# Layer one's values' pair and narrow gate pair side by side, both by seven products

## The chip, the core and the metric

The kernel runs on one core of one Trainium2 chip. The metric is the device time of one execution in microseconds (us), the median of the runs. Engine names are those of the profile: PE is the matmul engine (PEld its weight loads), DVE the vector engine, ACT the scalar engine, POOL and SP two engines that here mostly issue transfers.

## The reference

Two layers of a hybrid streaming encoder on 512 tokens of width 2048, all in float32. The changed part is the input projection of the first layer: some column blocks of `h @ w_in`.

```python
def hybrid_layer(x, w_in, w_out, g_pre, g_post, w_alpha, b_alpha, g_gla, g_att, rel_bias):
    h = rmsnorm(x, g_pre)
    z = h @ w_in
    gq, gk, gv, gg, ga, aq, ak, av, ag = split_columns(z)
    log_a = jax.nn.log_sigmoid((ga @ w_alpha + b_alpha).astype(jnp.float32)) / GLA_TAU
    ...
    o_att = chunk_band_attention(aq..., ak..., av..., rel_bias)
    o_att = rmsnorm(o_att, g_att...) * jax.nn.silu(ag)
    y = jnp.concatenate([o_gla, o_att], axis=-1) @ w_out
    return x + rmsnorm(y, g_post)
```

`av` (1024 columns) are the attention's values, `ag` (1024 columns) its gates, `ga` (16 columns) feed the forget gate.

## The kernel before

**Tiling.** The inner dimension of 2048 is cut into 8 chunks of 256 (two weight rows of 128, index `kk`), the tokens into 4 tiles of 128. The gates `ag` are one full block AG0 of 512 columns and two narrow blocks AG1 and AG2 of 264, where AG2 also holds the 16 columns of `ga`. The values are the two blocks AV0 and AV1 of 512 columns.

**Two words per operand.** Each operand is kept as a high half (a rounded copy, made by ACT: `wh`, line 240, for weights; line 109 for tokens) and a low half (the rest, made by DVE: `wl`, line 250; line 110). A product is three matmuls, high x high, high x low, low x high.

**Two ways to multiply.** `std_gemm` multiplies a block directly. `fast_gemm` takes a pair of blocks and uses seven products P1 to P7 in place of eight (the Strassen-Winograd scheme): the tokens are cut into quarters A11, A12, A21, A22 (half of the tokens x half of the inner dimension), the weights into the pair's two blocks x the same halves. Sums S1 to S4 of the token quarters (`token_sums`, `make_sums`) and sums of weights are the operands of P5, P6, P3 and P7; P1, P2 and P4 use A11, A12 and A22. Each product runs over 4 chunks `c`; a line such as `PROD` lists the order, "50" being P5 of chunk 0.

**Layer one's order.** AG0 by `std_gemm` on the raw tokens; then AG1 and AG2 by `std_gemm`, while the token sums are made and written to DRAM; then the values' pair by `fast_gemm`, which fetches the sums back; then the query/key pairs QK01/QK23 and QK45/QK67. In layer two AG0 is cut in half, the values' pair is begun between the halves, and AG1/AG2 already go by seven products as `GATE_PAIR`.

**The stream.** All weights pass through one list, `stream`, of jobs (one product, one chunk). Three steps run ahead of the matmuls: `load` (a transfer issued by SP), `high` (DVE's sum or difference of weights if needed, then ACT's copy) and `low` (DVE). `ahead()` says how far: five loads, four high halves, three low halves. The tile rings behind them are `raw` (5 tiles), `wh` (4), `wl` (3) and `H` and `sa` (4 each). Each engine executes its own queue in order; waits are semaphores between engines. A transfer, too, waits in its issuer's queue until its tile is free.

**Side work.** `first_operands` makes the normed tokens and A11, A12, A21, A22 out of the raw ones (line 719 and `split`); generators in `tasks` are advanced between matmuls by `pump`, at a rate per product. `gate_evac` applies silu and writes gates to DRAM from POOL's queue.

Of the kernel before, what the change touches and what calls it, by code (L numbers as in the profile page):

```python
# [15 lines left out]
P = 128  # L16
L = 2
# [19 lines left out]
def hybrid_trunk(  # L37
# [113 lines left out]
    class Job:  # L151
        def __init__(self, l, kind, c, b0, b1=None, pair=None):
            self.l, self.kind, self.c, self.b0, self.b1, self.pair = l, kind, c, b0, b1, pair
            self.a = None
            self.parted = l == L - 1 and kind != "std" and b0 == AV0
# [18 lines left out]

        def load(self):
# [10 lines left out]
            elif k == "P1":  # L186
                h = slot(f"g{4 + c}", [2, 512]) if self.parted else rtile("H")
                p["H", self.c] = self.fetch(h, b0, top)
                last_h[0] = last_load[0]
            elif k == "P5" and self.parted:  # L190
                h = p["H", c]
                src = w[self.l, b1 - (b1 > AG1), top].rearrange("p (k n) -> p k n", k=2)
                nc.gpsimd.dma_start(h, src, accum_op=ALU.add)
            elif k == "P5":
                p["r", self.c] = self.fetch(rtile("raw", bufs=5), b1, top)
            elif k == "P6":
                p["r", self.c] = p["b22", self.c] = self.fetch(rtile("raw", bufs=5), b1, bottom)
            elif k == "P7":
                p["r", self.c] = p.pop(("t", self.c), None) or self.fetch(rtile("raw", bufs=5), b0, top)
            elif k == "P2" or (k == "P4" and (end or self.parted)):  # L200
                p["r", self.c] = self.fetch(rtile("raw", bufs=5), b0, bottom)
            sums = (so_d if end else sa_d)[self.l]
# [3 lines left out]
            else:  # L206
                home = k == "P5" and b0 == AV0
            if b0 == AG1 and k == "P5":
                p["a22", c] = slot(f"g{4 + c}", [2, 512], F32R)
                nc.sync.dma_start(flat(p["a22", c]), sums["A22", c])  # L210
            if b0 == AG1 and k == "P3":
                p["next"]["H", c] = self.fetch(slot(("g14", "g15", "g2", "g12")[c], [2, 512]), PAIRS[1][0], c)
            if b0 == AG1 and k == "P4":
                self.a = p["a22", c]
            elif src is not None and b0 != NB_IN and not home:
                until(lambda: k == "P4" or (id(sums), LEFT[k], c) in written)
                self.a = rtile("sa", (2, 512), F32R)
                with tc.issue_after(last_h[0]) if mid else nullcontext():
                    last_load[0] = nc.sync.dma_start(flat(self.a), src).ins
            if b0 == W23[0] and k == ("P6" if mid else "P5"):  # L220
# [3 lines left out]
        def high(self):  # L224
# [3 lines left out]
            else:  # L228
# [3 lines left out]
                with tc.issue_after(lows[-4 if early else -2]) if self.b0 >= NB_IN else nullcontext():  # L232
                    if k == "P6" or (k == "P5" and not self.parted) or (k == "P4" and (self.b0 >= NB_IN or self.parted)):
# [25 lines left out]
    for l in range(L):  # L259
        if l:  # L260
            pr = {}
            stream += [Job(l, "std", c, AG0) for c in CO]
# [3 lines left out]
            qk = {}  # L266
            pr = {"next": qk}
            stream += [Job(l, k, c, *GATE_PAIR, pr) for k, c in PROD_GATE]
        else:
            stream += [Job(l, "std", c, b) for b in (AG0, AG1, AG2) for c in CO]  # L270
        for b0, b1 in PAIRS[1:] if l else PAIRS:
            pr = qk if l and b0 == QK01 else {}
# [29 lines left out]
    written = set()  # L302

# [36 lines left out]
    def std_gemm(l, blk, outs, chunks, operand, evac, rate=0.0, skip=0, lag=0):  # L340
        wide = W if blk == AG0 else N1
        pss = {o: ps_mm.tile([P, W], F32, tag="mm", name=nm("mm"))[:, :wide] for o in outs}
# [29 lines left out]
    def fast_gemm(l, pair, consume, rate=0.0, skip=0, feature_major=False, after=None, end=False, lag=0, ops=A, prod=None, acc=None):  # L372
        b0 = pair[0]
        gates = b0 == AG1
        wide = N1 if gates else W
        parted = acc is not None
        if not parted:
# [6 lines left out]
        if parted:  # L384
            target.update(P5="Z", P3="Z")
        if prod is None:
# [4 lines left out]
        def copies(name, src):  # L391
            keep[name] = []
            for t in range(2):
                e = ev()[:, :wide]
# [9 lines left out]
        def finished(k, t):  # L404
# [8 lines left out]
            elif k == "P2":  # L413
                consume(0, 0, t, None, combine(acc[target[k]][t], keep["p1"][t], ALU.add, keep["p1"][t]))
            elif k == "P4":
# [35 lines left out]
        for k, c in prod:  # L451
            if k == "P2" and (end or gates) and c == 0 or k == "P5" and parted and c == 0:
                acc["Z"] = [aux()[:, :wide], aux()[:, :wide]]
            if lag and k == "P4" and c == 4 - lag:
                held = [take(l, b0, k, i) for i in range(c, 4)]
                for t in range(2):
                    with tc.issue_after(last_mm[0]) if t else nullcontext():
                        for i in range(c, 4):
                            matmuls(held[i - c], k, i, (t,))
                            pace()  # L460
                    finished(k, t)
                return
            job = take(l, b0, k, c)
            with tc.issue_after(half_turns[1]) if (k, c) == ("P4", 3) and half_turns else nullcontext():
                matmuls(job, k, c, range(2))
            ahead()
# [16 lines left out]
            pace()  # L483

# [26 lines left out]
    STAGE = ("g6", "g7", "g4", "g5", "g10")  # L511
    HOME = {("S1", c): tag for c, tag in enumerate(("g9", "g14", "g15", "g2"))}
    HOMES = {**HOME, **{("S2", c): tag for c, tag in enumerate(("g12", "g13", "g8", "g11"))}}
# [94 lines left out]
    def make_sums(dst, tags, parts, home={}):  # L608
        stage = [0]

        def sub(out, a, b):
            nc.vector.tensor_tensor(out=out, in0=a, in1=b, op=ALU.subtract)
# [13 lines left out]
        for c in range(4):  # L626
            a11, a12, a21, a22 = parts(c)
            yield
            sub(a22, a21, a22)
            put("S1", c, a22)  # L630
            yield
            sub(a21, a11, a21)
            put("S3", c, a21)
            yield
            nc.vector.tensor_tensor(out=a22, in0=a22, in1=a11, op=ALU.subtract)
            put("S2", c, a22)
            yield
            nc.vector.tensor_tensor(out=a12, in0=a12, in1=a22, op=ALU.add)
            put("S4", c, a12)
            yield  # L640

    def token_sums(l):
        tags, home = (("g10", "g16", "H", "g0", "g1"), HOMES) if l else (STAGE, HOME)
        return make_sums(sa_d[l], tags, lambda c: (full[0, c][:, 0, :], full[0, c][:, 1, :], full[1, c][:, 0, :], full[1, c][:, 1, :]), home)

    VT = ("g16", "g17", "g4", "g5", "g6", "g7", "g12", "g13")
# [59 lines left out]
    def first_operands():  # L706
        ends = []
        for ch in CO:
            kh, c = divmod(ch, 4)
            while ch not in U:  # L710
                yield
            for half in range(2):
# [4 lines left out]
                with tc.issue_after(ends[-2]) if len(ends) >= 2 else nullcontext():  # L717
                    for kk in range(2):
                        nc.vector.scalar_tensor_tensor(
                            out=dst[:, kk * 256 : (kk + 1) * 256], in0=V[ch][:, kk, tok],  # L720
                            scalar=gcol[:, 2 * ch + kk : 2 * ch + kk + 1], in1=rb[:, tok], op0=ALU.mult, op1=ALU.mult,
                        )
                if half == 0:
                    op = slot(f"a1{kh + 1}{c}", [2, 512], F32R)
                elif kh == 0:
                    op = slot(A21[c], [2, 512], F32R)
# [5 lines left out]
                if half and kh:  # L732
# [3 lines left out]
        yield from load_forget_gate(0)  # L736
# [26 lines left out]
    def load_forget_gate(l):  # L763
        raw = slot("g10" if l else "g12", [2, 512])
        fac = slot("g13", [2, 512], F32R)
# [829 lines left out]
```

## Time and profile before

| What | Value |
| --- | --- |
| Median of 3 runs | 1592.07 us (1591.72 to 1592.32) |
| The profiled execution's own time | 1594.45 us |
| Its span in the trace | 1592.7 us |
| Granted clock of PE | 0.999 |
| Narrow matmuls (264 columns) of both layers | 720 |
| First narrow gate matmul starts | 50.80 us |
| Values' pair ends, query/key pair begins | 176.68 us |
| DMA, mean over the span | 277 GB/s |

The page gives each engine's busy time and its share of the span, then the chain of work that ended last: followed back from the last instruction, at each step to what released it. Busy time of PE alone does not say how fast it works, since matmuls are pipelined: one that takes 0.28 us may be followed by the next after 0.12. So the distance from start to start is used for prices. Stretches of the trace give busy time by engine between two times.

### The profile page before, as it was taken

The page shows a single profiled execution, that of the slowest core. Times are in us where ns is not written, and L with a number is a line of the kernel's source. Part 1 is how long each engine was busy: PE and PEld are TensorE (multiplying, and loading weights), DVE is VectorE, ACT ScalarE, POOL GpSimd, SP SyncE. Part 2 cuts the span into 40 slices and gives each one's busy share as a digit, 9 for nine tenths or more (in the row PEclk, how much of TensorE's full clock was granted, in tenths as well). Part 3 has the DMA queues.
Part 4 walks back from the last instruction along what each step waited for, and adds up shares of the span by engine and source line. Part 5 has one row for each costly group of instructions (what it writes and reads, how often), then busy time and mean ns, then how long its engine had stood idle before and what let it go on. Part 6 is the DMA issues. An engine that isn't in the chain of part 4 may idle for free.

```text
span 1592.7 us, 25038 instructions
## 1 busy us (share of the span) xinstructions
PE 1578.6 (99%) x9102; PEld 1369.3 (86%) x9102; DVE 1277.0 (80%) x1697; ACT 920.0 (58%) x1535; POOL 130.8 (8%) x222
## 2 busy tenths in 40 slices
PE   9999999999999999999999999999999999999998
PEld 7998999998888777888888899999988887778886
DVE  5978768678687878998989878775886878699887
ACT  7554445557465556664786456455574645476644
POOL 0220000000000000100122000000010000001001
PEclk9999999999999999999999999999999999999999
DMA  9698686685867869689889998847868597686887
GB/s 355 229 407 310 224 278 231 215 294 196 301 201 273 283 209 330 219 305 398 301 262 356 382 332 311 285 153 261 298 224 300 174 312 256 228 319 230 339 304 201
DMA packets 137739, 441.45 MB, mean 277 GB/s; under 512 B 15364, under 2 KB 27908, under 8 KB 137584
## 3 DMA queue, kind: packets, MB, share of 16 engines
q1 hardware_dynamic: 119952, 377.86, 67.5%
q0 software_dynamic: 17376, 61.70, 11.0%
q8 instruction: 72, 1.18, 0.3%
q14 instruction: 51, 0.42, 0.1%
q10 hardware_dynamic: 288, 0.30, 0.1%
HBM read 380.23 MB, written 61.62 MB: 277 GB/s over the span
## 4 chain that ended last, share of the span: by engine, by line
PE 86%; DVE 5%; DMA 5%; issue 2%; ACT 1%; SPq 0%; POOLq 0%; DVEq 0%; ACTq 0%
PE mm L445 51%; PE mm L435 17%; PE mm L358 6%; DMA raw<-in_w_dram 4%; PE ax L445 4%; DVE wl L250 2%; PE ax L1015 2%; PE ax L998 1%; PE ax L1204 1%; PE ax L1174 1%; PE ax L978 1%; PE ax L976 1%; PE ax L977 1%; ACT wh L240 1%; PE ax L1296 0%
## 5 line engine op out<-in xcount | busy, mean ns | idle before, releaser
L445 PE MATMUL mm<-wh,sa 128*128 128x512 f32 (+1 forms) x1600 | 501.1, 387 | 1.8 <-DMA sa<-S 1.3
L240 ACT CAST wh<-H 128x1024 fp32r<-128x1024 f32 (+1 forms) x240 | 245.2, 1024 | 191.9 <-PE mm L445 78.9
L445 PEld LDWEIGHTS mm<-wh,sa 128*128 128x128 f32 x1600 | 297.7, 188 | 64.9 <-ACT wh L240 3.0
L240 ACT CAST wh<-raw 128x1024 fp32r<-128x1024 f32 (+2 forms) x237 | 235.9, 1002 | 197.9 <-PE mm L445 87.4
L250 DVE TENSOR_TENSOR wl<-H,wh 128x1024 fp32r<-128x1024 f32 (+1 forms) x240 | 284.0, 1186 | 72.2 <-PE mm L445 25.4
L250 DVE TENSOR_TENSOR wl<-raw,wh 128x1024 fp32r<-128x1024 f32 (+2 forms) x237 | 272.5, 1154 | 49.3 <-PE mm L435 17.8
L445 PE MATMUL mm<-wl,sa 128*128 128x512 f32 (+1 forms) x800 | 310.1, 388 | 0.6 <-DVE wl L250 0.5
L435 PE MATMUL mm<-sa,wh 128*128 128x256 f32 x1280 | 237.8, 285 | 0.0
L445 PE MATMUL mm<-wh,a 128*128 128x512 f32 (+1 forms) x672 | 215.5, 387 | 0.0
L435 PEld LDWEIGHTS mm<-sa,wh 128*128 128x128 f32 x1280 | 200.3, 191 | 0.6
L435 PE MATMUL mm<-sa,wl 128*128 128x256 f32 x640 | 181.1, 284 | 0.5 <-DVE wl L250 0.5
L445 PEld LDWEIGHTS mm<-wl,sa 128*128 128x128 f32 x800 | 150.2, 188 | 31.9 <-DVE wl L250 2.3
L234 DVE TENSOR_TENSOR H<-H,raw 128x1024 f32<-128x1024 f32 (+1 forms) x136 | 160.8, 1185 | 1.6 <-DMA raw<-in_w_dram 1.0
L445 PEld LDWEIGHTS mm<-wh,a 128*128 128x128 f32 x672 | 125.2, 188 | 24.6
L445 PE MATMUL mm<-wl,a 128*128 128x512 f32 (+1 forms) x336 | 130.6, 389 | 0.5 <-DVE wl L250 0.5
L435 PEld LDWEIGHTS mm<-sa,wl 128*128 128x128 f32 x640 | 122.3, 191 | 0.9 <-DVE wl L250 0.9
L445 PE MATMUL mm<-wh,g 128*128 128x512 f32 (+1 forms) x416 | 120.4, 366 | 0.0
L236 DVE TENSOR_TENSOR raw<-H,raw 128x1024 f32<-128x1024 f32 (+1 forms) x52 | 61.5, 1182 | 48.4 <-DMA raw<-in_w_dram 48.3
L435 PE MATMUL mm<-a,wh 128*128 128x256 f32 x512 | 94.8, 285 | 0.0
L489 POOL TENSOR_TENSOR sm<-sm,mhalf 128x2 f32<-128x2 f32 (+2 forms) x40 | 38.0, 951 | 690.8 <-DVE sm L1025 367.1
L395 ACT COPY ev<-mm 128x512 f32<-128x512 f32 (+1 forms) x112 | 64.1, 573 | 52.8 <-PE mm L445 37.6
L445 PEld LDWEIGHTS mm<-wh,g 128*128 128x128 f32 x416 | 75.3, 188 | 13.4 <-ACT ev L395 0.6
(276 smaller groups left out, 2428.2 us busy)
## 6 DMA issues: line engine op xcount, KB each, us to landing
raw<-in_w_dram SPq DMA_DIRECT2D x287, 512.0 KB, 5.2
sa<-S SPq DMA_DIRECT2D x188, 512.0 KB, 4.7
H<-in_w_dram SPq DMA_DIRECT2D x56, 512.0 KB, 5.1
sa<-A SPq DMA_DIRECT2D x48, 512.0 KB, 6.3
sa<-oS SPq DMA_DIRECT2D x32, 512.0 KB, 5.7
S<-g POOLq DMA_DIRECT2D x30, 512.0 KB, 8.1
raw<-in_w_ag_dram SPq DMA_DIRECT2D x32, 264.0 KB, 4.3
oS<-g POOLq DMA_DIRECT2D x16, 512.0 KB, 4.8
```

Source lines behind the costliest of these rows:

```text
L234: nc.vector.tensor_tensor(out=h, in0=h, in1=r, op=ALU.add)
L236: nc.vector.tensor_tensor(out=r, in0=h, in1=r, op=ALU.subtract)
L240: last_cast[0] = nc.scalar.copy(self.wh[:, z, :], src[:, z, :]).ins
L250: last_low[0] = nc.vector.tensor_tensor(out=self.wl[:, z, :], in0=self.src[:, z, :], in1=self.wh[:, z, :].bitcast(F32), op=ALU.subtract).ins
L358: nc.tensor.matmul(pss[o], a(part, kk, o) if callable(a) else a[:, part, t], rhs[:, kk, :], start=(i == 0 and kk == 0 and m == 0), stop=(i ...
L395: last_copy[0] = nc.scalar.copy(e, src[t]).ins
L435: nc.tensor.matmul(dst, lhs[:, kk, f], a[:, part, tok], start=(fresh and kk == 0 and m == 0 and ft % 2 == 0), stop=(c == 3 and kk == 1 and ...
L445: last_mm[0] = nc.tensor.matmul(out_ps[t], a[:, part, tok], rhs[:, kk, :], start=(fresh and kk == 0 and m == 0), stop=(c == 3 and kk == 1 ...
L489: nc.gpsimd.tensor_tensor(out=out_r, in0=v, in1=mhalf[:, : v.shape[-1]], op=ALU.pow)
L976: nc.tensor.matmul(ps[:, :n], self.qh[:, t], self.kh[:, :n], start=True, stop=False)
L977: nc.tensor.matmul(ps[:, :n], self.qh[:, t], self.kl[:, :n], start=False, stop=False)
L1015: nc.tensor.matmul(o, self.pt[i][:, j * P : (j + 1) * P], av[hd // 4, j // 2][:, j % 2, (hd % 4) * P : (hd % 4 + 1) * P], start=(j == 0), ...
```

## The change

In layer one the two narrow gate blocks become a pair by seven products, as in layer two, and this pair and the values' pair run **side by side**: for each product and chunk of `PROD_TWIN` first the values' matmuls, then the gate's, on the same token operand. Both stand directly behind AG0.

- `first_operands` makes all of the first token half before the second, and starts when the matmuls have reached the full block's sixth chunk. A21 is not split any more, since no direct block needs it.
- The token sums are made in the order S1, then S2 and S4, then S3, in tiles of the ring `sa`, from which both pairs use them directly; each waits until the product four sums before it has been issued for the gate pair. They are still written to DRAM, for the later pairs. A22 is fetched back once and used by both pairs.
- The weight sums of P5 and P6 are made in the tile of P1's operand by a transfer that adds to its destination, issued by POOL, in place of a load and an addition on DVE. P6's second block is also loaded on its own, as the operand of P3. For P4 the first operand is restored on DVE out of a new load.
- The values' partial sums are six tiles of the pool `ps_mm`, two of them reused; the gate's are tiles of `ps_ax`. P4 gets its own accumulator and is added to what P7 left.
- The first operands of the first query/key pair are loaded ahead. The forget gate's preparation follows the block.

```diff
+    PROD_TWIN = order("20 21 22 23 10 11 12 13 50 51 52 53 60 30 61 31 62 32 63 33 70 71 72 73 40 41 42 43")
+    GATE_H = ("g8", "g11", "g9", "g10")
...
-            self.parted = l == L - 1 and kind != "std" and b0 == AV0
+            self.parted = kind != "std" and (b0 == AV0 or (b0 == AG1 and l == 0))
+            self.summed = self.parted and kind in (("P5",) if l else ("P5", "P6"))
...
+        def add(self, tile_, blk, c):
+            if blk == AG2:
+                nc.gpsimd.dma_start(flat(tile_)[:, : 2 * N1], w_ag[self.l, 1, c], accum_op=ALU.add)
+            else:
+                src = w[self.l, blk - (blk > AG1), c].rearrange("p (k n) -> p k n", k=2)
+                nc.gpsimd.dma_start(tile_, src, accum_op=ALU.add)
...
+            if self.summed:
+                self.add(p["tile", c], b1, top if k == "P5" else bottom)
...
-                    if k == "P6" or (k == "P5" and not self.parted) or (k == "P4" and (self.b0 >= NB_IN or self.parted)):
+                    if k in ("P5", "P6") and not self.summed or (k == "P4" and (self.b0 >= NB_IN or self.parted)):
                         nc.vector.tensor_tensor(out=h, in0=h, in1=r, op=ALU.add)
...
-            stream += [Job(l, "std", c, b) for b in (AG0, AG1, AG2) for c in CO]
+            stream += [Job(l, k, c, *z) for k, c in PROD_TWIN for z in ((*PAIRS[0], pr), (*GATE_PAIR, pg))]
...
+            elif l == 0:
+                op = A[name, c] = rtile("sa", (2, 512), F32R)
...
+            names = [("S1", c) for c in range(4)] + [(n, c) for c in range(4) for n in ("S2", "S4")]
+            names += [("S3", c) for c in range(4)]
+            left = {v: k for k, v in LEFT.items()}
+            for i, (name, c) in enumerate(names):
+                if i >= 4:
+                    n, c0 = names[i - 4]
+                    while (0, AG1, left[n], c0) not in issued:
+                        yield
+                make(name, c)
+                yield
...
+        while cursor[0] < 5:
+            yield
+        for half in range(2):
+            for ch in CO:
...
-            std_gemm(l, AG0, range(NT), CO, operand_raw, raw_evac, rate=0.25, lag=1)
-            tasks.append(token_sums(l))
-            std_gemm(l, AG1, range(NT), CO, operand_in, gate_evac(1), rate=1.0, lag=1)
-            std_gemm(l, AG2, range(NT), CO, operand_in, gate_evac(2), rate=1.0, lag=2)
-            drain()
...
-            fast_gemm(l, PAIRS[0], av_consume, rate=0.5)
+            std_gemm(l, AG0, range(NT), CO, operand_raw, raw_evac, rate=0.5, lag=1)
+            acc = {n: [ps_mm.tile([P, W], F32, tag="mm", name=nm("mm")) for _ in range(2)] for n in "YX"}
+            acc_g = {n: [aux()[:, :N1] for _ in range(2)] for n in "YX"}
+            twins = [
+                fast_gemm(l, pair, consume, rate=1, acc=z, steps=True)
+                for pair, consume, z in ((PAIRS[0], av_consume, acc), (GATE_PAIR, gate_consume, acc_g))
+            ]
+            tasks.append(token_sums(l))
+            for k, c in PROD_TWIN:
+                if (k, c) == ("P5", 0):
+                    acc["Z"] = [ps_mm.tile([P, W], F32, tag="mm", name=nm("mm")) for _ in range(2)]
+                for step in twins:
+                    step(k, c)
+            drain()
```

The change moves instructions in every queue. Three places follow, each as it stands in the program (source line, operation, output and inputs, shape); line numbers of the changed kernel are some 16 to 44 higher.

**DVE at the end of AG0.** `H` and `g14` hold normed tokens (line 719, 765 in the change), `a110`, `a120`, `a111`, `a121` are low halves of the first token half, `g9` and `g10` low halves of raw tokens (line 119), and `wl_85`, in the change `wl_82`, is the low half of AG0's last weight chunk. Before:

```order
L119 SCALAR_TENSOR_TENSOR g10_89_510<-g13_76_432,gcol_172,sa_88_509 128x512 x2
L110 TENSOR_TENSOR a110_60_342<-H_59_339,a110_60_342 128x512
L719 SCALAR_TENSOR_TENSOR H_59_339<-g17_11_207,gcol_172,bias_3_178 128x256 x2
L110 TENSOR_TENSOR g8_68_386<-g14_67_383,g8_68_386 128x512
L719 SCALAR_TENSOR_TENSOR g14_67_383<-g17_11_207,gcol_172,bias_3_178 128x256 x2
L250 TENSOR_TENSOR wl_85_503<-raw_74_425,wh_81_467 128x1024
L250 TENSOR_TENSOR wl_90_539<-raw_82_469,wh_86_505 128x528
```

In the change:

```order
L119 SCALAR_TENSOR_TENSOR g10_87_502<-g1_71_415,gcol_172,sa_86_501 128x512 x2
L110 TENSOR_TENSOR a110_81_475<-H_80_472,a110_81_475 128x512
L765 SCALAR_TENSOR_TENSOR H_88_519<-g0_17_223,gcol_172,bias_3_178 128x256 x2
L110 TENSOR_TENSOR a120_85_498<-H_80_472,a120_85_498 128x512
L765 SCALAR_TENSOR_TENSOR H_88_519<-g12_21_231,gcol_172,bias_3_178 128x256 x2
L110 TENSOR_TENSOR a111_89_522<-H_88_519,a111_89_522 128x512
L765 SCALAR_TENSOR_TENSOR H_94_560<-g13_25_239,gcol_172,bias_3_178 128x256 x2
L110 TENSOR_TENSOR a121_93_545<-H_88_519,a121_93_545 128x512
L765 SCALAR_TENSOR_TENSOR H_94_560<-g8_59_339,gcol_172,bias_3_178 128x256 x2
L266 TENSOR_TENSOR wl_82_490<-raw_70_413,wh_76_450 128x1024
```

The last chunk's low half stands behind four token rows more than before.

**POOL behind AG0.** `A22` and `S` are operands written to DRAM; `g4` to `g7` are the first weight operands of the values' pair, `g8`, `g11`, `g9`, `g10` those of the gate pair. Before, POOL only writes:

```order
L733 DMA A2201_99<-sa_116_674 128x1024
L733 DMA A2202_100<-sa_125_727 128x1024
L767 MEMSET g12_135_790 2x512
L623 DMA S100_82<-g9_140_821 128x1024
L623 DMA S300_90<-g6_141_832 128x1024
L623 DMA S301_91<-g5_148_888 128x1024
```

In the change:

```order
L781 DMA A2201_99<-sa_133_736 128x1024
L183 DMA g4_132_732<-in_w_dram 128x1024
L781 DMA A2202_100<-sa_141_781 128x1024
L781 DMA A2203_101<-sa_153_834 128x1024
L180 DMA g8_136_756<-in_w_ag_dram 128x528
L183 DMA g5_140_777<-in_w_dram 128x1024
L180 DMA g11_144_801<-in_w_ag_dram 128x528
L183 DMA g6_150_826<-in_w_dram 128x1024
L653 DMA S100_82<-sa_157_857 128x1024
L653 DMA S101_83<-sa_161_880 128x1024
```

The accumulating transfers of P5 (lines 180 and 183) stand between the write-backs, in one queue.

**DVE around P7.** Before, with one pair, the subtraction for P7 (line 236) of a chunk stands between low halves of wide weights:

```order
L236 TENSOR_TENSOR raw_247_1518<-H_187_1154,raw_247_1518 128x1024
L250 TENSOR_TENSOR wl_245_1514<-H_211_1325,wh_243_1498 128x1024
L250 TENSOR_TENSOR wl_249_1534<-raw_225_1411,wh_246_1516 128x1024
L250 TENSOR_TENSOR wl_252_1553<-raw_247_1518,wh_250_1537 128x1024
L236 TENSOR_TENSOR raw_254_1557<-H_190_1184,raw_254_1557 128x1024
```

In the change (line 252 is the subtraction, line 266 the low half, line 110 the split of a token sum; 528 is the gate's width):

```order
L252 TENSOR_TENSOR raw_251_1440<-g8_136_756,raw_251_1440 128x528
L266 TENSOR_TENSOR wl_240_1375<-g7_160_877,wh_238_1358 128x1024
L110 TENSOR_TENSOR sa_242_1380<-g14_121_668,sa_242_1380 128x512
L266 TENSOR_TENSOR wl_243_1396<-g10_164_900,wh_241_1377 128x528
L252 TENSOR_TENSOR raw_256_1463<-g5_140_777,raw_256_1463 128x1024
L266 TENSOR_TENSOR wl_245_1412<-raw_235_1336,wh_244_1398 128x1024
L110 TENSOR_TENSOR sa_248_1419<-g15_129_713,sa_248_1419 128x512
L266 TENSOR_TENSOR wl_249_1435<-raw_239_1360,wh_246_1414 128x528
L266 TENSOR_TENSOR wl_254_1458<-raw_247_1416,wh_250_1438 128x1024
L252 TENSOR_TENSOR raw_262_1491<-g11_144_801,raw_262_1491 128x528
```

The subtractions of both pairs now stand among low halves of both pairs and the splits of S3; `raw_262` is loaded when the low half of `raw_235` is done.

More of the change, by code (lines that the diff above doesn't have):

```diff
@@ L707, in first_operands @@
         ends = []
[L708 to L712, printed above, removed]
+        while cursor[0] < 5:
+            yield
+        for half in range(2):
+            for ch in CO:
+                kh, c = divmod(ch, 4)
+                while ch not in U:
+                    yield
                 if kh == 0:
```

165 lines of the change are left out of this document (92 added, 73 removed).

## The prediction

> **What bounds the kernel now.** I read the page's busy line and its chain first, then the stretches of the stage that is changed, then single rows.
>
> ```profile
> PE 1578.6 (99%) x9102; PEld 1369.3 (86%) x9102; DVE 1277.0 (80%) x1697; ACT 920.0 (58%) x1535; POOL 130.8 (8%) x222
> PE 86%; DVE 5%; DMA 5%; issue 2%; ACT 1%; SPq 0%; POOLq 0%; DVEq 0%; ACTq 0%
> ...
> 50.70:100.60 49.90, 48.93 (x390) 47.74 (x389) 46.61 (x88) 28.83 (x52) 14.97 (x28) 1.00 0.91 328
> 100.60:176.70 76.10, 76.10 (x340) 62.82 (x339) 58.10 (x57) 34.42 (x38) 1.67 (x3) 1.00 0.89 329
> ```
>
> TensorE is busy for 99% of the span and 86% of the chain that ended last. A matmul less is therefore time less, as long as its operands keep up. The two stretches are layer one's narrow gate blocks and its values' pair (columns: length, busy time of PE, weight loads, DVE, ACT, POOL, then granted clock, DMA share, GB/s). In the first DVE is busy too, 46.61 of 49.90 us; in the second it has 18 us to spare. The DMA engines are 0.9 full in both, the clock is 1.00.
>
> What a matmul costs is its distance to the next one:
>
> ```profile
> 50.80 0.28 PE L358 MATMUL mm<-wh,a 128*128 128x264 f32 x1
> ...
> 58.08 0.28 PE L358 MATMUL mm<-wh,g 128*128 128x264 f32 x1
> ...
> 59.42 0.28 PE L358 MATMUL mm<-wh,g 128*128 128x264 f32 x1
> ...
> 108.65 68.03 PE mm L445 x300
> 176.68 33.04 PE mm L435 x276
> ```
>
> Eleven narrow matmuls start from 58.08 to 59.42: 0.122 us each. Three hundred wide ones take 68.03: 0.227 each.
>
> **The change, part by part.**
>
> *The matmuls.* The gate blocks were 2 blocks x 8 chunks x 4 token tiles x 6 = 384 narrow matmuls. Seven products of 4 chunks x 2 tiles x 6 make 336. The values' 336 wide ones stay. 48 x 0.122 = **5.9 us less**. The recorded order confirms the 48; that the change leaves them in is no possibility.
>
> *Waits that go.* From 50.80 to 176.68 are 125.9 us. 384 x 0.122 = 46.8 and 336 x 0.227 = 76.3 explain 123.1; 0.4 are forget-gate transposes and about 0.4 early query/key matmuls, both moved and kept. **2.0 us** are waits of the old gate blocks, which the new block replaces by its own.
>
> *DVE at the block's beginning.* Prices, again start to start:
>
> ```profile
> 35.24 1.22 DVE L250 TENSOR_TENSOR wl<-raw,wh 128x1024 fp32r<-128x1024 f32 x1
> 36.38 0.87 DVE L719 SCALAR_TENSOR_TENSOR H<-g,gcol,bias 128x256 f32<-128x256 f32 x2
> 37.17 0.87 DVE L719 SCALAR_TENSOR_TENSOR g<-g,gcol,bias 128x256 f32<-128x256 f32 x2
> 37.96 2.73 DVE L119 SCALAR_TENSOR_TENSOR g<-g,gcol,sa 128x512 fp32r<-128x512 f32 x4
> 40.61 0.68 DVE L110 TENSOR_TENSOR a<-H,a 128x512 fp32r<-128x512 f32 x1
> ...
> 47.94 0.70 DVE L250 TENSOR_TENSOR wl<-raw,wh 128x528 fp32r<-128x528 f32 x1
> 48.56 0.69 DVE L612 TENSOR_TENSOR g<-g 128x512 f32<-128x512 f32 x1
> 49.16 0.69 DVE L110 TENSOR_TENSOR a<-H,a 128x512 fp32r<-128x512 f32 x1
> 49.77 0.88 DVE L719 SCALAR_TENSOR_TENSOR H<-g,gcol,bias 128x256 f32<-128x256 f32 x2
> ```
>
> So a wide low half (1024) is 1.14, a narrow one (528) 0.62, a 512 row 0.60, a pair of L719 0.79, four of L119 2.65. In the new order the low half of the full block's last chunk stands behind the four raw-token rows (2.65), six pairs (4.75) and four splits (2.4) from 36.38 on: 9.8 + 1.14, done at 47.3. PE wants it when that chunk's second group starts:
>
> ```profile
> 45.36 1.07 PE L358 MATMUL mm<-wh,sa 128*128 128x512 f32 x4
> 46.27 0.39 PE L358 MATMUL mm<-wl,sa 128*128 128x512 f32 x1
> ```
>
> At 46.27, so PE waits **1.1 us** and ends the full block at 51.9 instead of 50.8. From there I added DVE's rows against PE's twelve wide (2.72 us) and twelve narrow matmuls (1.46 us) per step. The second value product's low half is done at 56.8, when PE reaches it; the four steps of P2 then have 1 to 2 us of lead. Before the gate's first P1 half stand nine rows of token sums (5.0 us): it is done at 73.1 and wanted at 72.0, and the next wide one 0.3 late. **1.4 us** more; 2.5 in all here. These sums do not wait for PE, so nothing else hides them; if ACT's casts, which interleave with them, come one cast (1.0 us) later each time, it is 4.5, and if DVE starts the tokens earlier it is 0.5.
>
> *The middle.* A step is 4.18 us of PE. DVE has 1.76 of low halves, 0.6 to 1.2 of sums and splits: it gains 1 us a step until the three buffers of low halves stop it, about 3 us ahead. Of DVE's own work the block has 100 us in 117 us of PE.
>
> *The accumulating transfers.* P5 and P6 no longer add on DVE but by a transfer into the first operand's tile. Its issue waits for the low half of the product before, in POOL's queue behind the operands' write-backs. Layer two has four such:
>
> ```profile
> L193 POOL DMA_DIRECT2D g<-in_w_dram x4: 859/862/910, 830.9 to 842.4; - x4
> ...
> DMA to landing us min/median/max: 5.5/7.6/10.0
> ...
> 843.00:845.00 2.00, 2.00 (x11) 1.65 (x10) 2.00 (x4) 0.34 (x2) 0.80 (x2) 1.00 0.97 201
> 900.00:930.00 30.00, 29.53 (x152) 25.21 (x151) 22.47 (x26) 13.03 (x18) 0.00 (x0) 1.00 0.97 376
> ```
>
> P1 and P5 of a chunk lie four steps apart, 16.7 us. Issue 0.9, landing 7.6, cast 1.0, low half 1.1 leave 6 us: hidden, **0**. Behind a waiting accumulation stand the write-backs of S1 and the next chunks' accumulations, which are later still. On SP one load of the third pair (into a ring tile that S4 of chunk 0 must leave, by my sum at 98) stands ahead of a P3 load that can't go before 104: nothing either. The cover is thin: full DMA engines move only 201 GB/s while accumulating, 376 otherwise.
>
> *P7 and P4.* Both now use two raw buffers a step out of the same five. A load goes out when the low half five raws earlier is done, and DVE stands in front of its subtraction:
>
> ```profile
> raw<-in_w_dram SPq DMA_DIRECT2D x22, 512.0 KB, 6.7
> raw<-in_w_ag_dram SPq DMA_DIRECT2D x8, 264.0 KB, 3.9
> ```
>
> By my sum the gate's first P7 load leaves at 121.5 and lands at 125.4, but DVE reaches its subtraction at 123.8: 1.6 late, and 1.9 when the buffers repeat two products on. With splits, P3's combinations and gate copies between, the fifth low half from there (value chunk 2 of P7) is done at 147.1 and wanted at 146.1 to 146.3: PE waits **1.0**; a narrow load taking the wide one's 6.7 makes it 4.1, none late 0.5. I take 1.4, near the narrow row. P4 repeats the loop with DVE 1 us ahead: 0; its operand A22, now fetched back behind P7's in the same ring, has three steps, 12 us, to land. Later stages stand in nearly the same order as before: 0, give or take 1.
>
> *The sum.* -5.9 - 2.0 + 2.5 + 1.4 = **-4.0 us**. The profiled execution took 1594.45 us, 1.75 more than its span; it becomes 1590.4. The median of the runs shown is 2.4 below it, so 1592.07 - 4.0 = **1588.1**.
>
> A row and a rule: the narrow load's median was 3.9 us, the wide one's 6.7. The Trainium skill, "DMA: Bandwidth & Descriptors", section "Anatomy of one DMA", fits one transfer on the software path by 2.0 us plus its bytes at 436 GB/s. That is an estimate of 2.6 and 3.2 us here, with which P7's wait would be near 0.5 and the sum -4.9. The trace is well above the fit, since 0.9 of the DMA engines are taken.
>
> **The rivals.**
>
> *Nothing waits anew in P7, and less at the beginning.* If loads land before DVE asks (below 2.3 us for the narrow ones) and DVE is a microsecond earlier at the start, -5.9 - 2.0 + 1.5 + 0.5: 1586.2. DVE's 100 us in 117 speak for it, a DMA share of 0.9 against. The fit above would give this result.
>
> *DVE's queue becomes the bound.* The beginning at 4.5 and P7 at 4.1 give +0.7, so 1592.8; half of each excess, 1590.5. For it: the old gate stretch, where DVE was 93% busy and PE waited. Against: DVE's lead in the middle.
>
> *The accumulations come late, and it is slower.* Between 67 and 104 us P5 and P6 move 8 x 512 KiB and 8 x 264 KiB this way, 6.4 MB, at 201 GB/s 32 us of all engines; write-backs and loads of some 5.8 MB at 376 GB/s take 15. That is 47 us of work in 37: P6's first tiles come up to 10 us late against 6 us of slack. PE then waits 4 us once, and as much again if P5 is late already: 1592 to 1596. From 6 us of lateness on it decides, and above 7 us of waits the kernel is slower. Against it: each accumulation waits for DVE anyway, so they spread out, and later chunks of P6 have two steps each.
>
> **How the numbers follow.** A change under 0.2%, 3.2 us, can't be told from none here; 1588.9 and 1595.3 are the borders. Forecast 0.45, on either side of 1588.1 by 2 (0.36 faster, 0.09 same); no new wait 0.16 (faster); DVE's queue 0.22 (same); late accumulations 0.17 (0.15 slower, 0.02 same). Faster 0.52, same 0.33, slower 0.15. The range runs from 1585.0, below which all waits would have to vanish, to 1594.0; above it lies most of the last rival.
>
> **What would show it.** The narrow matmuls of layer one should number 336. The low half of the full block's last chunk should end near 47.3, PE's wait there near 1.1. The last value product should end near 172.7 instead of 176.7. Idle of PE ended by DVE's low halves at P1's first gate chunk and in P7 is as forecast; idle ended by ACT's cast of an accumulated tile, with landings above 13 us, is the slow rival. The forecast is wrong if the beginning, which I know only to 2 us either way, or the query/key stage, which I took as unchanged, moves by as much as the gain.

## The result, and the profile after

The changed kernel takes **1603.05 us** (median of 4 runs, 1599.69 to 1606.86) against 1591.89 for the kernel before: ratio 1.0073, 95% interval 1.0049 to 1.0096. It is slower by 11 us, where 4 us of gain were forecast. Five more runs gave 1602.65 (1.0070, 1.0058 to 1.0082).

The page of the changed kernel, its busy line and its chain by engine:

```profile
PE 1577.2 (99%) x9054; PEld 1366.3 (86%) x9054; DVE 1281.1 (80%) x1715; ACT 926.6 (58%) x1551; POOL 147.3 (9%) x238
PE 88%; DMA 5%; DVE 4%; ACT 2%; issue 1%; SPq 0%; POOLq 0%; DVEq 0%; ACTq 0%
```

The 48 matmuls are gone (9102 before, 9054 now). Little else on the page tells of a loss: a matmul at half clock counts as busy. The block shows it, here in stretches (columns as in the prediction):

```profile
51.80:71.30 19.50, 19.50 (x109) 16.88 (x107) 19.50 (x35) 10.09 (x16) 3.92 (x8) 1.00 0.96 331
71.30:84.00 12.70, 5.84 (x21) 4.90 (x20) 5.42 (x8) 4.73 (x7) 3.17 (x4) 0.61 0.94 260
84.00:90.00 6.00, 6.00 (x32) 5.12 (x32) 5.10 (x8) 2.73 (x4) 3.56 (x6) 0.97 1.05 186
90.00:142.20 52.20, 52.19 (x301) 45.86 (x300) 34.29 (x45) 29.70 (x44) 15.22 (x23) 1.00 1.00 302
142.20:150.00 7.80, 5.30 (x20) 4.00 (x19) 6.93 (x9) 2.44 (x6) 1.07 (x2) 0.78 0.74 240
150.00:184.70 34.70, 34.70 (x203) 30.61 (x203) 31.94 (x52) 17.19 (x26) 3.24 (x6) 1.00 0.98 368
```

PE stands still in two of them, and in both the granted clock is low, 0.61 and 0.78. From 84 to 90 the DMA engines are full (1.05) and move 186 GB/s. The block ends at 184.7, where the first query/key matmul starts. By the same measure it ended at 176.5 before (the 176.68 of the table ahead is the start of the chain's row), and 4.0 less, 172.5, was forecast. PE's waits of the change there:

```profile
PE ax L467 <- ACT wh L256: 6.7, 1, 6.7
PE mm L467 <- DVE wl L266: 2.5, 1, 2.5
```

Each is one event. The chain of waits leads from the first to a transfer:

```profile
64.61 0.80 DVE g L765 x2
65.42 0.02 issue
65.43 12.08 DMA g<-in_w_ag_dram
77.51 0.02 issue
...
77.59 0.64 ACT wh L256
...
78.25 0.72 DVE wl L266
...
79.22 1.22 PE mm L467 x2
80.44 2.64 PE ax L467 x12
83.08 3.42 PE mm L467 x12
```

The gate pair's first P1 operand goes into tile `g8`. Its previous tenant is a chunk of raw tokens, which `first_operands` reads for the last time at 65.4. Only then does SP issue the load, and it lands 12.1 us later. Behind it twelve narrow matmuls take 2.64 us where 12 x 0.122 = 1.46 is the price, and twelve wide ones 3.42 for 2.72. The granted clock is 0.50 from 74.1 to 84.4 us, and again from 145.8 to 149.2:

```profile
74.20:84.30 10.10, 5.89 (x20) 5.10 (x21) 4.85 (x7) 4.73 (x7) 2.95 (x4) 0.50 0.90 253
145.80:149.20 3.40, 3.40 (x10) 2.61 (x9) 3.03 (x5) 0.00 (x0) 0.53 (x1) 0.50 0.95 265
```

PE works again from 78.3 on, so 6.1 us of the first stretch are run at half speed: some 3 us more.

The second wait hangs on two loads of P7, and the ten wide matmuls behind it take 4.09 us for 10 x 0.227 = 2.27:

```profile
125.03 0.10 DVE wl L266
...
125.14 8.50 DMA raw<-in_w_dram
...
135.49 0.63 DVE wl L266
...
136.14 6.47 DMA raw<-in_w_dram
...
143.85 1.23 DVE wl L266
145.08 0.04 issue
145.12 4.09 PE mm L467 x10
```

SP's queue around them (issue, length, line, transfer):

```profile
115.24 0.33 SPq L175 DMA_DIRECT2D H<-in_w_dram  x1
115.86 1.30 SPq L175 DMA_DIRECT2D raw<-in_w_dram  x1
...
124.52 0.33 SPq L175 DMA_DIRECT2D H<-in_w_dram  x1
125.14 0.77 SPq L175 DMA_DIRECT2D raw<-in_w_dram  x1
...
135.52 0.33 SPq L175 DMA_DIRECT2D H<-in_w_dram  x1
136.14 0.33 SPq L175 DMA_DIRECT2D raw<-in_w_dram  x1
```

Three raw loads leave 0.62 us behind an H load. The H loads belong to the third pair, far later; each waits at the queue's head for a token sum to leave its ring tile (SP has six waits for such sums between 66 and 150 us, 46.5 us in all). It looks like a blocked queue, and this is one of the theories below. The chain says otherwise: the low half that frees the raw tile ends at 125.12 and 136.12, and the load leaves 0.02 us later. What sets these loads is DVE's work and their own landing of 8.5 and 6.5 us, not their place behind the H loads.

### The profile page after: what moved, and what is told of

It is laid out like the page before. It is cut to its first block, busy times and chain, and to the rows that moved or that the text cites. A ratio compares the mean times of both kernels' runs of the same rounds, so it can differ in the third digit from the quotient of the medians.

```text
span 1597.9 us, 25010 instructions
## 1 busy us (share of the span) xinstructions
PE 1577.2 (99%) x9054; PEld 1366.3 (86%) x9054; DVE 1281.1 (80%) x1715; ACT 926.6 (58%) x1551; POOL 147.3 (9%) x238
## 4 chain that ended last, share of the span: by engine, by line
PE 88%; DMA 5%; DVE 4%; ACT 2%; issue 1%; SPq 0%; POOLq 0%; DVEq 0%; ACTq 0%
PE mm L467 50%; PE mm L457 20%; PE ax L467 6%; PE mm L374 4%; DMA raw<-in_w_dram 2%; PE ax L1069 2%; DVE wl L266 2%; PE ax L1052 1%; PE ax L1258 1%; DMA sa<-S 1%; DMA g<-in_w_ag_dram 1%; PE ax L1228 1%; PE ax L1032 1%; PE ax L1031 1%; PE ax L1030 1%
## 5 line engine op out<-in xcount | busy, mean ns | idle before, releaser
L467 PE MATMUL mm<-wh,sa 128*128 128x512 f32 (+1 forms) x1632 | 514.1, 388 | 1.3 <-DMA sa<-S 0.7
L467 PEld LDWEIGHTS mm<-wh,sa 128*128 128x128 f32 x1632 | 303.9, 188 | 65.3 <-issue 1.8
L467 PE MATMUL mm<-wl,sa 128*128 128x512 f32 (+1 forms) x816 | 317.4, 389 | 4.3 <-DVE wl L266 4.3
L256 ACT CAST wh<-H 128x1024 fp32r<-128x1024 f32 (+1 forms) x208 | 211.9, 1020 | 162.6 <-PE mm L467 68.8
L266 DVE TENSOR_TENSOR wl<-H,wh 128x1024 fp32r<-128x1024 f32 (+1 forms) x208 | 245.6, 1182 | 53.3 <-PE mm L467 22.7
L467 PEld LDWEIGHTS mm<-wl,sa 128*128 128x128 f32 x816 | 153.5, 188 | 36.0 <-DVE wl L266 6.3
L457 PE MATMUL mm<-sa,wl 128*128 128x256 f32 x640 | 180.4, 283 | 0.0
L250 DVE TENSOR_TENSOR H<-H,raw 128x1024 f32<-128x1024 f32 (+1 forms) x120 | 141.5, 1183 | 0.3
L256 ACT CAST wh<-g 128x1024 fp32r<-128x1024 f32 x84 | 81.0, 974 | 76.9 <-DVE g L250 27.5
L266 DVE TENSOR_TENSOR wl<-g,wh 128x1024 fp32r<-128x1024 f32 x84 | 93.9, 1122 | 31.3 <-PE mm L457 8.5
L467 PE MATMUL mm<-wh,g 128*128 128x512 f32 (+1 forms) x384 | 109.9, 364 | 0.0
L415 ACT COPY ev<-mm 128x512 f32<-128x512 f32 (+1 forms) x112 | 64.1, 573 | 46.5 <-PE mm L467 32.5
```

The source lines that it names most:

```text
L250: nc.vector.tensor_tensor(out=h, in0=h, in1=r, op=ALU.add)
L256: last_cast[0] = nc.scalar.copy(self.wh[:, z, :], src[:, z, :]).ins
L266: last_low[0] = nc.vector.tensor_tensor(out=self.wl[:, z, :], in0=self.src[:, z, :], in1=self.wh[:, z, :].bitcast(F32), op=ALU.subtract).ins
L415: last_copy[0] = nc.scalar.copy(e, src[t]).ins
L457: nc.tensor.matmul(dst, lhs[:, kk, f], a[:, part, tok], start=(fresh and kk == 0 and m == 0 and ft % 2 == 0), stop=(c == 3 and kk == 1 and ...
L467: last_mm[0] = nc.tensor.matmul(out_ps[t], a[:, part, tok], rhs[:, kk, :], start=(fresh and kk == 0 and m == 0), stop=(c == 3 and kk == 1 ...
```

## The experiments

Three suspects: a **late operand** (`g8`), a **blocked queue** (the H loads on SP), and **DMA time** (accumulating transfers, which fill the engines at about half the bytes). Times are medians; "block ends" is the start of the query/key matmuls in the run's profiled execution (176.5 before the change). One profile is one execution: what lies behind the block is nearly the same program in all of them and takes 1410.5 to 1418.5 us, so a block's end can't be set against a median to the microsecond. The verdicts go by the medians.

| Run | Median us | Ratio to before, 95% | Block ends |
| --- | --- | --- | --- |
| e0_after | 1602.65 | 1.0070 (1.0058 to 1.0082) | 186.8 |
| e1_order | 1601.93 | 1.0059 (1.0046 to 1.0072) | 182.9 |
| e2_fill | 1602.50 | 1.0077 (1.0064 to 1.0090) | 187.7 |
| e3_noacc | 1601.11 | 1.0054 (1.0039 to 1.0069) | 183.3 |
| e4_hold | 1600.44 | 1.0066 (1.0052 to 1.0080) | 184.7 |
| e5_order_hold | 1596.16 | 1.0038 (1.0025 to 1.0050) | 180.4 |
| e6_p6dve | 1602.00 | 1.0072 (1.0059 to 1.0084) | 186.6 |
| e7_order_hold_p6 | 1591.75 | 1.0002 (0.9994 to 1.0011) | 174.8 |
| e8_hold2 | 1595.93 | 1.0029 (1.0018 to 1.0039) | 178.9 |
| e9_p7ring | 1594.69 | 1.0031 (1.0017 to 1.0045) | 176.8 |
| e10_order_p6 | 1595.63 | 1.0031 (1.0020 to 1.0043) | 179.9 |
| e11_noacc_dve | 1598.59 | 1.0058 (1.0046 to 1.0070) | 181.2 |
| e12_hold_p6 | 1599.01 | 1.0042 (1.0030 to 1.0054) | 180.9 |
| e13_wb_sp | 1600.03 | 1.0055 (1.0041 to 1.0069) | 182.2 |
| e14_a22_sp | 1599.77 | 1.0051 (1.0039 to 1.0063) | 184.1 |
| e15_late_b22 | 1597.01 | 1.0037 (1.0025 to 1.0049) | 178.8 |
| e16_gate_p5 | 1596.21 | 1.0032 (1.0019 to 1.0044) | 176.8 |
| e18_best_again | 1591.55 | 0.9999 (0.9990 to 1.0008) | 173.7 |

**The change again.**

> The changed kernel once more, as the measure for the runs beside it. Theory (late operand): its first gate P1 operand, tile g8, is loaded only when the xT chunk in g8 has been read for the last time (65.4 us), lands after 12.1 us, TensorE waits 6.9 us for it at 71, and the granted clock then falls to 0.5 to 0.7 until 84 us, 3.2 us more; a second wait of 2.7 us at 142 with 1.7 us of lower clock behind it. All of this is expected again, 1600 to 1607 us, with the first wait anywhere between 5 and 10 us. Rival (a disturbed stretch of one execution): a profile without the wait at 71.

The wait at 71 came again, 7.1 us long, with the half clock behind it. It belongs to the kernel. The second wait came as 2.1 us at 145, this time at full clock.

**The late operand alone.**

```diff
-    GATE_H = ("g8", "g11", "g9", "g10")
+    GATE_H = ("g9", "g10", "g11", "g8")
```

> Only the order of the gate pair's P1 tiles changes: chunks 0 to 3 go to g9, g10, g11, g8 in place of g8, g11, g9, g10, so that the first one waits only for the end of the raw operands (about 52 us) and not for the xT chunk in g8. Theory (late operand): the wait at 71 and the low clock behind it go, 6.9 + 3.2 = 10 us less than the changed kernel, 1592 to 1595 us, with 1 us or less of wait on TensorE between 70 and 80; the wait at 142 stays. Rival (DMA traffic as such, with the accumulating adds in it): the next load is late in its turn, 1600 us or more, with a wait of 4 us or more somewhere between 70 and 90.

The wait at 71 is gone and the time is not. PE's waits between 50 and 185, and pieces of the chain:

```profile
PE ax L467 <- DVE wl L266: 3.1, 1, 3.1
PE mm L467 <- DVE wl L266: 3.1, 2, 2.6
PE ax L467 <- ACT wh L256: 2.1, 1, 2.1
```

```profile
73.36 12.63 DMA A<-sa
...
86.59 12.09 DMA g<-in_w_ag_dram
...
101.69 12.51 DMA S<-sa
```

Now a write-back of A22, an accumulation and a write-back of S land after 12 us each; a token sum needs the `sa` tile that the write-back holds. The first theory, a single late operand, fell here.

**PE kept busy in the wait.** Ahead of the gate's first P1 step:

```diff
+                        for i in range(52):
+                            nc.tensor.matmul(
+                                acc_g["X"][0], A[0, 0, 0][:, 0, 0:P], z.wh[:, 0, 0:N1], start=True, stop=True,
+                            )
```

> Changed kernel with 52 narrow matmuls (52 x 0.122 = 6.3 us) of no use ahead of the gate pair's first P1, into the accumulator that this P1 then starts afresh; they run while TensorE would wait for g8. Theory (the wait itself lowers the clock afterwards): first useful gate P1 matmul with its low half still at 79 us, but the granted clock stays at 0.95 or more between 72 and 90 us, so some 3 us less than the changed kernel. Rival (the clock falls there for a reason of its own): the clock falls to 0.5 to 0.7 all the same, no gain. Rival (the wait isn't set by a landing but by work on TensorE's way): the fillers come on top, 6 us more.

The stretches 72 to 84 of this kernel; the change had PEclk 0.61 from 71.3 to 84.0:

```profile
72.00:78.00 6.00, 5.79 (x45) 5.43 (x43) 0.21 (x2) 0.79 (x2) 0.00 (x0) 1.00 1.03 335
78.00:84.00 6.00, 5.64 (x33) 4.75 (x34) 6.00 (x9) 4.64 (x7) 4.28 (x6) 1.00 0.79 169
```

The clock stays at 1.00, so its fall is the wait's doing. The 3 us are not gained: another wait, 4.3 us, appears at 131, with 3.4 us of half clock behind it. PE's speed did not bound this stage.

**The gate's accumulations left out.**

```diff
-            if self.summed:
+            if self.summed and self.b0 != AG1:
```

> Changed kernel with the eight accumulating loads of the gate pair (P5 and P6) left out, so the gate columns are computed from P1's weights alone in P5 and P6; the values' eight stay. Theory (late operand): the g8 load is ahead of them, so the wait at 71 stays and the time is within 2 us of the changed kernel. Rival (the accumulating transfers are what is late or what fills the DMA): 1596 us or less, with no wait of 3 us or more left.

Within 2 us of the change, as the late operand had it, with the wait at 71 at 7.3 us. Its load stands ahead of all accumulations of the gate.

**The blocked queue, P6's sum, and the three edits together.** The H loads behind the loads that precede them in the program:

```diff
-                p["H", self.c] = self.fetch(h, b0, top)
+                with tc.issue_after(last_load[0]) if b0 == QK45 and not self.l else nullcontext():
+                    p["H", self.c] = self.fetch(h, b0, top)
```

P6's sum on DVE, from the tile that P3 needs anyway:

```diff
-            self.summed = self.parted and kind in (("P5",) if l else ("P5", "P6"))
+            self.summed = self.parted and kind == "P5"
```

> Changed kernel with only the four early H loads of the third pair (issued on SyncE at 106.5, 115.2, 124.5 and 135.5 us, each after a wait for a token sum) put behind the loads that stand ahead of them in the program. Theory (SyncE's queue is blocked): P7's loads, which left 0.6 us behind these H loads, leave when the ring frees them, the wait at 142 and the low clock behind it (2.7 + 1.7 us) go, 1597 to 1600 us. Rival (DMA time): the P7 transfers are late for lack of DMA time, not of a place in the queue, within 2 us of the changed kernel (1602.6).

> Tile order g9, g10, g11, g8 and the H loads held back. Theory (two separate waits, a late operand and a blocked queue): 6.9 + 3.2 + 4.4 us less than the changed kernel, 1588 to 1590 us. Rival (DMA time: accumulating packets at half rate and the write-backs of the sums on POOL's queue fill the DMA engines from 66 to 130 us, so that the next transfer is late when one wait is taken away): 1597 us or more, with waits of 2 us or more between 84 and 130 us and a DMA share of 1.0 or more from 70 to 130 us.

> Changed kernel with P6's second sum made by VectorE from the tile that P3 loads anyway (8 adds, 4 x 1.14 + 4 x 0.62 = 7 us of VectorE), in place of eight accumulating transfers. The tile order stays, so the wait at 71 stays. Rival (DMA time): some 16 us of DMA engine time go from the stage, the queue is shorter from 95 us on, and the waits after 100 us go: 1597 to 1600 us. Theory (late operand and blocked queue only): the waits at 71 and 142 both stay, within 2 us of the changed kernel, or later where VectorE is the next bound.

> All three edits. DMA time theory: with 16 us of DMA engine time less and the first operand early, less than 3 us of waits are left between 50 and 175 us, 1586 to 1590 us, faster than the kernel before. Late operand and blocked queue only: the same as with the first two edits. VectorE as the next bound: 1592 us or more, with TensorE waiting for VectorE's adds or low halves in P6.

Alone, holding the H loads back is worth 2.2 us by the medians and P6's sum 0.7, but their ratios to the kernel before, 1.0066 and 1.0072 beside 1.0070, do not tell them from nothing. Tile order and held H loads together are worth 6.5, about half of what two separate waits would give; all three 10.9. What P6's eight accumulations cost is seen between e5 and e7. First e5, its stretches and two rows of its transfers from 60 to 130 us (KB each, median us from issue to landing), then the same of e7:

```profile
100.00:115.00 15.00, 15.00 (x85) 13.12 (x85) 8.93 (x11) 9.54 (x15) 5.38 (x8) 1.00 1.07 260
115.00:130.00 15.00, 10.84 (x64) 9.10 (x62) 6.00 (x7) 6.93 (x10) 1.06 (x2) 1.00 0.79 291
```

```profile
S<-sa POOLq DMA_DIRECT2D x11, 512.0 KB, 12.1
raw<-in_w_ag_dram SPq DMA_DIRECT2D x4, 264.0 KB, 7.7
```

```profile
100.00:115.00 15.00, 14.94 (x87) 12.92 (x86) 12.64 (x16) 9.79 (x16) 2.13 (x4) 1.00 0.53 196
115.00:130.00 15.00, 15.00 (x88) 13.27 (x87) 11.25 (x15) 7.60 (x10) 1.61 (x3) 1.00 0.64 206
```

```profile
S<-sa POOLq DMA_DIRECT2D x12, 512.0 KB, 4.8
raw<-in_w_ag_dram SPq DMA_DIRECT2D x5, 264.0 KB, 4.5
```

The DMA share falls from 1.07 to 0.53, the write-backs land in 4.8 us instead of 12.1, and DVE has room for the adds (12.64 of 15). The forecast of 1586 to 1590 for all three was missed by 2. In the profiles the block ends 1.7 us earlier than before the change, yet the medians agree; but the profiled execution of the kernel before, 1594.45 us, was longer than every other run of it (1588.67 to 1593.60).

**Each edit as the last one.** e10 lacks the held H loads, e12 the tile order.

> Tile order and P6's sum on VectorE, the H loads not held back. Tells whether the blocked queue still costs where DMA time is free: theory with three causes: 1594 to 1597 us, between the changed kernel and all three edits (1591.75), with waits of 2 us or more behind the H loads between 120 and 150 us. Rival (the queue matters only while the DMA engines are full): 1592 us, the same as all three.

> H loads held back and P6's sum on VectorE, the tile order as in the changed kernel. Theory (three causes that cover one another): the wait at 71 of about 7 us and the low clock behind it stay, DMA time is free after 95 us, so the loss is not made up: 1598 to 1602 us, 7 us or more above all three edits (1591.75). Rival (the tile order only moves a wait about): 1594 us or less.

Put in last, the tile order is worth 7.3 us (1599.0 to 1591.75), P6's sum 4.4, the held H loads 3.9, each beyond the intervals; put in first, 0.7, 0.7 and 2.2, none clear of noise. So each edit counts, and each hides the others: that the DMA engines use one wait to catch up on the next fits this, but no run shows it by itself. Both theories that left one edit out fell.

For two of the edits the rows show the cause: the wait at 71, still 5.1 us in e12, and the DMA time of P6's sums. For the H loads they don't. In e10, too, each wide raw load leaves only when the low half has freed its tile, so the blocked queue is not it. DMA time fits in part: the third wide P7 load lands after 7.1 us in e10, where it follows an H load, and after 5.2 in e7. But e10's wait at 85, 3.2 us against 1.4 in e7, comes before its first H load leaves at 104.8, and no run separates the H loads' transfers from their place. What the 3.9 us are made of stays open.

**What is left.** Four tries to better the three edits. e8 moves the next pair's early loads behind P7's, e9 puts the gate's P7 loads into the H ring as well, e11 moves P5's sums to DVE too, on top of e8; e16 only the gate pair's, on top of e7; the first two lines below are e11's.

```diff
-            self.summed = self.parted and kind in (("P5",) if l else ("P5", "P6"))
+            self.summed = self.parted and kind == "P5" and l > 0
...
-            if b0 == AG1 and k == ("P3" if self.l or c < 2 else "P4"):
+            if b0 == AG1 and k == ("P3" if self.l else "P7" if c < 2 else "P4"):
...
-                p["r", self.c] = p.pop(("t", self.c), None) or self.fetch(rtile("raw", bufs=5), b0, top)
+                p["r", self.c] = z or self.fetch(rtile("H") if own else rtile("raw", bufs=5), b0, top)
...
-            elif k == "P5" and not self.parted:
+            elif k == "P5" and not self.summed:
```

> The three edits (tile order, H loads held back, P6's sum on VectorE) and, beside them, the loads of the next pair's first two operands (g12, g13, 2 x 1.3 us of DMA time at 54 to 64 us, wanted at 175) moved behind P7's loads. DMA time theory: the write-backs of A22 land sooner in the full stretch from 66 to 90 us, the wait of 1.5 us at 84 (a sum's tile waits for such a write-back) shrinks to under 0.8, some 1 us less than the three edits (1591.75). Rival (that wait is POOL's or VectorE's): no difference.

> As the run before, and the gate pair's four P7 loads go into the H ring, which is free by then, so that the ring of five raw tiles serves only the values' P7 and both P4. Ring theory (with the DMA no longer full after 100 us, the waits of about 1 us at 147 and 161 come from a ring of five: tile free, load of 5 to 8 us, subtraction, cast, low half): these waits go, 1 to 2 us less than the run before. Rival (a load in the H ring waits for the token sum of its tile and stands ahead of the raw loads on SyncE): a new wait at 120 to 140 us, no gain or a loss of up to 3 us.

> As the first run of this group, with P5's sums on VectorE as well, so that no accumulating transfer is left in this stage of layer one: 8 more raw loads and 8 more adds (7 us of VectorE). DMA time theory: another 8 us of DMA time less before 115 us, 1588 to 1591 us. Rival (VectorE and the raw ring are the next bound there, VectorE was busy over 0.9 of 90 to 100 us): 1593 us or more, with TensorE waiting for low halves between 85 and 115 us.

> All three edits, and the gate pair's P5 sums on VectorE too (4 more raw loads of 1.4 us of DMA time, 4 adds of 0.62 us), so that only the values' P5 accumulates by transfers. DMA time theory: 3 us of DMA time less before 100 us, the wait at 84 shrinks below 1 us, 1590 to 1591 us. Rival (VectorE is the next bound at 80 to 100 us, as where all of P5 was moved to it): 1593 us or more, with waits for low halves between 85 and 105 us.

> The three edits once more, beside the run above: 1591.7 us, within 0.2% of the kernel before.

None helps. In e8 the wait at 84 shrinks to 0.8, but P7's loads are late again (2.4 us at 143); e9 has 4.5 us of waits from 84 to 160. PE's waits from 50 us on add up to 6.0 us in e8 against 3.5 in e7, and its block ends 4.1 us later than e7's; the rest of its loss stays open. e16 goes the way of its rival, with 3.8 us of waits for low halves, most of them later than it said. Without any accumulation (e11) DVE is next, as that rival had it; PE's waits there:

```profile
PE ax L469 <- DVE wl L268: 3.2, 3, 1.8
PE mm L469 <- DVE wl L268: 2.9, 6, 1.0
```

The last question was why write-backs take 12 us between 66 and 90 even in e7. e13 and e14 move all, or only A22's, to SP's queue; e15 also puts P6's first loads behind them.

```diff
-                    nc.gpsimd.dma_start(sa_d[0]["A22", c], flat(op))
+                    nc.sync.dma_start(sa_d[0]["A22", c], flat(op))
...
-            nc.gpsimd.dma_start(dst[name, c], flat(op))
+            (nc.gpsimd if l else nc.sync).dma_start(dst[name, c], flat(op))
```

> All three edits, and all twenty write-backs of layer one's sums on SyncE's queue, which issues nothing from 69 to 107 us, in place of POOL's. Theory (POOL's issuing delays them): the write-back that the wait at 84 hangs on lands 3 us or more sooner, the wait goes, 1 to 2 us less than all three edits (1591.75). Rival (DMA engines' time): same landing, no gain; and the write-backs stand ahead of P7's raw loads on SyncE, up to 3 us more.

> As the run before with only the four write-backs of A22 on SyncE, so that nothing new stands ahead of P7's loads. Theory (POOL's issuing): 1 to 2 us less than all three edits. Rival (DMA engines' time): within 1 us of them, the wait at 84 stays over 1 us.

> As the run before, and P6's first five raw loads (2.1 MB, some 5.3 us of DMA time, issued at 60 to 66 us and wanted from 104 us on) stand behind A22's write-backs on SyncE. DMA engines' time: the write-backs land 4 us or more sooner, the wait at 84 goes, 1 to 2 us less than all three edits, 1590 us. Rival (POOL's issuing or VectorE's queue sets that wait): no difference to the run before.

Leaving POOL's queue makes them later, not sooner (11.95 us in e7, 17.05 in e14, 18.69 in e13). The chain of e14, then that of e15:

```profile
68.82 17.05 DMA A<-sa
```

```profile
84.87 15.58 DMA g<-in_w_ag_dram
```

POOL's issuing is not what delays them. In e15 the wait at 84 is gone, and an accumulation of P5 lands after 15.6 us instead, with 2.4 us of waits for casts from 88 to 106. That fits full DMA engines; how they share their time between the two queues was not tried.

## Why the prediction was wrong

*The matmuls* (-5.9): right, 48 fewer. *The full block's end* (1.1): right in size; it ends at 51.8 instead of 50.8, behind a wait of 0.5 us.

*The gate's first P1* (1.4): **the step that failed most**. It took DVE's rows as what ends last, and the operand as landed. The wait was 6.7, ended by a transfer of 12.1 us whose tile came free late. The load that has to follow that tile's last reader, at 65.4, was no term of the sum; I read only DVE's queue.

*The clock*: the prediction noted 1.00 and gave no price to a wait beyond its length. Behind 6.7 and 2.5 us of wait came some 3.0 and 1.8 us more.

*The accumulating transfers* (0): wrong. They were hidden themselves, but their DMA time made others late; P6's alone cost 4.4 us with the other two mended. The slow rival had the resource right, "47 us of work in 37", and the victim and size wrong: not P6's tiles, but a load, the write-backs and through them the token sums.

*P7* (1.4): the mechanism, the raw ring, was there; the size was 2.5, and 1.8 of clock. *"On SP one load of the third pair"* was priced at nothing. As a place in the queue that was right, for all four such loads; but holding them back is worth 3.9 us once the other two edits are in, by a cause that stays open.

Against the forecast end at 172.5 these are 5.3 (6.7 for 1.4), 3.0, 1.1 (2.5 for 1.4) and 1.8: 11.2 of the 12.2 us. With the three edits the block ends at 174.8 and 173.7, near the forecast. Why the median then only equals that of the kernel before, the runs do not settle; the one profile of that kernel shows its longest execution, so its block may end earlier in the others.

## What to carry to other kernels

When an operand gets a tile that something else held, find that tenant's last reader and add a landing at the DMA load of that moment, before looking at any engine's queue. Adding in the transfer frees the vector engine but not the DMA engines: sum their time over the stage, write-backs included. And where several waits cover one another, mend them together before judging any: singly, these three edits looked like nothing.

## What the runs showed of the hardware

Full DMA engines do not always move the same: 415 GB/s at a share of 1.02 before the change,

```profile
90.00:100.00 10.00, 10.00 (x83) 9.96 (x83) 6.92 (x17) 5.68 (x9) 2.69 (x5) 1.00 1.02 415
```

but 186 at 1.05 while accumulating (84 to 90 us above). The prediction's rule of 2.0 us plus bytes at 436 GB/s gave an estimate of 2.6 us for 264 KiB (the Trainium skill, "DMA: Bandwidth & Descriptors", section "Anatomy of one DMA"). That fit is of the software path; here such a load, issued by SP while the engines were 0.94 full or more, took 12.1.

The clock fell to half not only after the 6.7-us wait, but after 2.5 us, and in e10 after 1.8, while waits of 2.1 (e1) and 2.4 (e8) left it at 1.00. Each stretch at half clock in the block lasted 3.4 us, or twice or three times that: 10.2 and 3.4 in the change, 6.8 in e3 and e12, 3.4 in e10. So one such stretch under running matmuls costs 1.7 us, half of its length, however short the wait was. Stretches of e10 around its wait:

```profile
138.00:140.00 2.00, 0.28 (x2) 0.00 (x0) 2.00 (x3) 1.43 (x4) 0.00 (x0) 1.00 0.31 125
140.00:142.00 2.00, 1.90 (x5) 1.52 (x6) 2.00 (x4) 0.00 (x0) 0.53 (x1) 0.58 0.38 97
142.00:144.00 2.00, 2.00 (x7) 1.59 (x6) 1.59 (x3) 0.00 (x0) 0.00 (x0) 0.57 1.09 315
144.00:146.00 2.00, 2.00 (x16) 1.88 (x15) 2.00 (x5) 1.40 (x2) 0.53 (x1) 1.00 0.90 332
```

The Trainium skill ("TensorE: Matmul & The Clock Gate", section "Part 1: The HAM clock gate") says that the clock halves after an idle window of some 3.4 us that runs freely. The length of the stretches agrees with it, and a phase of its own would explain why 1.8 us can cost and 2.4 not; that less than a whole window suffices differs from it.
